# Second attention of a two-block transformer: wider score products, one compressed product, values' products of a query tile in one run

## The chip, the cores and the metric

The kernel runs on one core of a Trainium2 chip. Its time is the device time of one execution in microseconds (us); the median of several executions is given. The core's engines run beside each other and meet at semaphores: TensorE (matrix products; PE in the profile, PEld its weight loads), VectorE (DVE), ScalarE (ACT), GpSimd (POOL) and SyncE (SP, which issues transfers).

## The reference, cut to what matters

Two transformer blocks on 512 tokens of width 1024, in float32. The first block (two attentions, a mixture of experts) is not touched. The second mixes a causal convolution with an attention of 16 heads in 4 groups of 4 heads; each group shares its keys and values, 64 wide. Each head has three branches, weighted by sigmoid gates: compressed keys (31 blocks), selected blocks and a window. With 512 tokens the selection and the window both come to plain causal attention over all earlier tokens, with keys and values of their own:

```python
g = jax.nn.sigmoid(gate_logits).reshape(B, S, 3, G, R, 1)
o = g[:, :, 0] * o_cmp + g[:, :, 1] * o_slc + g[:, :, 2] * o_win
```

where `o_slc` and `o_win` are, for each head, softmax(q k^T / 8 + bias of the distance, masked) v.

## The kernel before, in words

The function `mixer` holds the second block's mixing. It normalises the input (`two_norms`), projects it with weights that arrive by DMA and are split into a high and a low part (`load_w`, lines 94 to 100: one transfer, one ACT and one DVE instruction), and multiplies with three products per 128 features (`mm3`, lines 84 to 86; in the trace `pz<-hh,whi`, `pz<-hl,whi`, `pz<-hh,wlo`, 512 columns each). These projections give queries, keys, values, gates and the inputs of the convolution. The convolution is done on DVE as 31 taps for each of 8 channel tiles (`taps`, lines 1490 and 1492), a few at a time between other work.

The attention loop (lines 1685 to 1707) goes over 8 units u: group g = u // 2 and pair pr = u % 2 of its heads. `k_stacks` writes the keys of two groups as stacked high and low parts, `KS[b][g][x]`, each 128 x 512, for branch b (0 selected, 1 window); it runs before unit 0 and again before unit 4, into the same memory. `cmp_branch` makes the compressed branch's probabilities `cpT` for a group. `attend` (line 1631) then works through four query tiles t of 128 tokens, with n = 128 (t + 1) visible keys, and yields after each one, so that taps, a gate of the convolution, a gate of the attention or the next group's queries are put in between in the program. In one tile:

- Scores: for each branch b and head i two products (lines 1643 and 1644) of n columns into a PSUM tile `sc` (two such tiles); DVE adds the bias and takes the minimum (line 1646) into `probs[b]`; ACT takes the exponential and its sum (line 1648). `probs` has one tile for each branch with two buffers each.
- In a block of raised priority, DVE turns sums and gates into factors (lines 1651 to 1654). Two products a tile (line 1658) put the compressed values into the output `po`, one for each head, in plain fp32 and of 128 columns.
- Then for each branch: for each head ACT scales the probabilities (line 1664), TensorE transposes their t + 1 blocks into a PSUM tile `tr` (line 1667; two such tiles), ACT copies them out to `aT` (line 1669; four buffers); then the branch's 2 (t + 1) products of values (line 1673), plain fp32, add to `po`. Head 0 writes rows 0 to 63 of `po`, head 1 rows 64 to 127.

After tile 3 DVE copies `po` out (line 1677); there is one `po`.

Nobody writes the order of an engine's instructions by hand. It is fixed when the kernel is built: of the instructions whose inputs are ready by its estimates, an engine takes the one that comes first in the program, and `high_priority(30)` moves a block's instructions ahead by 30 places. Each engine then runs its list in that order and waits where a semaphore is not yet there. `issue_after(x)` adds to that the rule that the block's instructions on the engine of x come behind x.

Of the kernel before, what the change touches and what calls it, by code (L numbers as in the profile page):

```python
# [1433 lines left out]
def mixer(K, X, vecd, gain, mem, pre, mem_done, wp):  # L1434
# [5 lines left out]
    with ExitStack() as st:  # L1440
# [56 lines left out]
        with ExitStack() as sk:  # L1497
# [5 lines left out]
            KS = [[None] * 4 for b in range(2)]  # L1503
# [6 lines left out]
            def k_stacks(j):  # L1510
                for b, c0 in ((0, 3584), (1, 4096)):
                    pz = proj(c0 + P * j)
                    for i in range(2):
                        KS[b][2 * j + i] = [kv.tile([P, S], F32R, tag=f"K{b}{i}{x}", bufs=1, name=K.uid("K")) for x in range(2)]
                        stack_k(K, pz, i, *KS[b][2 * j + i])
                    early()
# [114 lines left out]
            def attend(g, pr, qs, bt, cpT):  # L1631
                po = pso.tile([P, S], F32, tag="po", name=K.uid("po"))
                for t in range(NT):
# [3 lines left out]
                    probs = [wk.tile([P, 2, S], F32, tag=f"p{i}", name=K.uid("p")) for i in range(2)]  # L1637
                    m = wk.tile([P, 2, 2, 2], F32, tag="am", name=K.uid("am"))
                    for b in range(2):
                        for i in range(2):  # L1640
                            r = 2 * pr + i
                            sc = psc.tile([P, S], F32, tag="sc", name=K.uid("sc"))
                            nc.tensor.matmul(sc[:, :n], qs[r][:, ts_], KS[b][g][0][:, :n], start=True, stop=False)  # L1643
                            nc.tensor.matmul(sc[:, :n], qs[r][:, ts_], KS[b][g][1][:, :n], start=False, stop=True)  # L1644
                            p = probs[b][:, i, :n]
                            v.tensor_tensor_reduce(p, sc[:, :n], bt[r][:, b0:b0 + n], scale=1.0, scalar=3e38,  # L1646
                                                   op0=OP.add, op1=OP.min, accum_out=m[:, 0, b, i:i + 1])
                            nc.scalar.activation(p, p, AF.Exp, scale=-1.0, bias=m[:, 0, b, i:i + 1],  # L1648
                                                 accum_out=m[:, 1, b, i:i + 1])
                    with K.tc.high_priority(30):  # L1650
# [5 lines left out]
                        for i in range(2):  # L1656
                            r = 2 * pr + i
                            nc.tensor.matmul(po[64 * i:64 * i + 64, ts_], vcz[:, g, r, :], cpT[:, ts_], start=(t == 0),  # L1658
                                             stop=False, skip_group_check=True)
                        for b in range(2):  # L1660
                            pts = []
                            for i in range(2):
                                p = probs[b][:, i, :n]
                                nc.scalar.activation(p, p, AF.Copy, scale=m[:, 1, b, i:i + 1])  # L1664
                                pt = pst.tile([P, NT, P], F32, tag="tr", name=K.uid("tr"))
                                for k in range(t + 1):
                                    nc.tensor.transpose(pt[:, k, :], p[:, k * P:(k + 1) * P], K.ident)  # L1667
                                x = wk.tile([P, NT, P], F32, tag="aT", bufs=4, name=K.uid("aT"))
                                nc.scalar.activation(x[:, :t + 1], pt[:, :t + 1], AF.Copy)
                                pts.append(x)  # L1670
                            for k in range(t + 1):
                                for i in range(2):
                                    nc.tensor.matmul(po[64 * i:64 * i + 64, ts_], V[b][:, k, 64 * g:64 * g + 64],  # L1673
                                                     pts[i][:, k, :], start=False, stop=(b == 1 and k == t and t == NT - 1),
                                                     skip_group_check=True)
# [299 lines left out]
```

## Time and profile before

| what | value |
|---|---|
| median of 3 runs | 1972.51 us |
| lowest and highest | 1968.85 and 1977.4 us |
| the profiled execution's own time | 1969.21 us |
| its span, first to last instruction | 1967.4 us |
| mean granted TensorE clock | 0.989 of full speed |
| busy: TensorE products, DVE, ACT, POOL | 1907.5, 1093.7, 770.4, 156.3 us |

The profile comes from one execution. Busy time of TensorE counts every product from its start to a modelled end, and those overlap, so it says when TensorE had something in flight and not how full it was. What a product takes of TensorE's time is read from the distance between starts in the timeline.

### The profile page before, as it was taken

Reading aid. Unit: us, or ns where it says so; the run is one execution under the profiler, and the core shown is the slowest. Engines: PE = TensorE matmul, PEld = TensorE weight load, DVE = VectorE, ACT = ScalarE, POOL = GpSimd, SP = SyncE. Lnnn points to the kernel's source line nnn. Section 1 sums busy time; section 2 is a strip of 40 time slices with the busy share of each in tenths; the row PEclk is TensorE's granted clock in tenths of the full one; section 3 lists DMA queues with packets and bytes.
Section 4 is the critical chain, followed back from the end, with each engine's and each line's share of the span. In section 5 each row is a group of like instructions: output and inputs, shape, how many; then the busy total and the mean of one; then the engine's idle time right before and its main releaser. Section 6 shows DMA issues by size and latency. Waiting matters only on the chain.

```text
span 1967.4 us, 26583 instructions
## 1 busy us (share of the span) xinstructions
PE 1907.5 (97%) x10370; PEld 1395.2 (71%) x10370; DVE 1093.7 (56%) x1965; ACT 770.4 (39%) x1602; POOL 156.3 (8%) x226
## 2 busy tenths in 40 slices
PE   7999998899999999989999999999999999999998
PEld 5786678545455554548777777777898898888886
DVE  6876753722332223246998989747555544444423
ACT  5435653221112211124236776786344443332321
POOL 0111000000000000000011101101100001111000
PEclk8999999999999999999999999999999999999999
DMA  9854054699999999953332122202342133333322
GB/s 308 305 181 146 1 200 177 237 412 405 419 402 422 413 404 408 426 177 87 97 108 54 54 55 65 55 22 75 97 130 85 47 93 97 97 97 96 126 78 86
DMA packets 210327, 356.38 MB, mean 181 GB/s; under 512 B 18742, under 2 KB 160434, under 8 KB 185624
## 3 DMA queue, kind: packets, MB, share of 16 engines
q1 hardware_dynamic: 207168, 346.81, 48.7%
q0 software_dynamic: 2768, 7.75, 1.3%
q8 instruction: 83, 1.36, 0.3%
q14 instruction: 44, 0.36, 0.1%
q10 hardware_dynamic: 264, 0.10, 0.0%
HBM read 350.37 MB, written 9.49 MB: 183 GB/s over the span
## 4 chain that ended last, share of the span: by engine, by line
PE 47%; DVE 6%; issue 1%; ACT 1%; DMA 0%; POOL 0%; DVEq 0%; POOLq 0%; SPq 0%; ACTq 0%
PE pz L86 12%; PE pz L85 12%; PE pz L84 12%; PE po L1673 3%; PE tr L1667 2%; DVE cva L1492 2%; DVE wlo L100 1%; PE sc L1643 1%; PE sc L1644 1%; PE po L1658 0%; DMA xkr<-xkd 0%; PE tr L1328 0%; PE tr L1277 0%; DVE q L241 0%; DVE K L251 0%
## 5 line engine op out<-in xcount | busy, mean ns | idle before, releaser
L84 PE MATMUL pz<-hh,whi 128*128 128x512 f32 x912 | 362.8, 398 | 1.9 <-DVE cblk L1397 0.8
L86 PE MATMUL pz<-hh,wlo 128*128 128x512 f32 x912 | 360.4, 396 | 0.7 <-DVE wlo L100 0.7
L85 PE MATMUL pz<-hl,whi 128*128 128x512 f32 x912 | 359.7, 395 | 0.0
L99 ACT ACTIVATE whi<-raw 128x1024 fp32r<-128x1024 f32 (+2 forms) x166 | 181.2, 1096 | 346.1 <-PE pz L85 254.1
L100 DVE TENSOR_TENSOR wlo<-raw,whi 128x1024 fp32r<-128x1024 f32 (+2 forms) x166 | 219.5, 1326 | 77.9 <-ACT whi L99 77.6
L1094 PE MATMUL eg<-ew,xg 128*64 128x512 f32 x1024 | 224.3, 593 | 0.0
L84 PEld LDWEIGHTS pz<-hh,whi 128*128 128x128 f32 x912 | 171.4, 188 | 38.4 <-issue 2.1
L86 PEld LDWEIGHTS pz<-hh,wlo 128*128 128x128 f32 x912 | 171.6, 188 | 37.2 <-issue 2.1
L85 PEld LDWEIGHTS pz<-hl,whi 128*128 128x128 f32 x912 | 171.6, 188 | 35.3 <-issue 2.5
L1492 DVE SCALAR_TENSOR_TENSOR cva<-cv,cvp,cva 128x512 f32<-128x512 f32 x240 | 179.1, 758 | 4.2
L1094 PEld LDWEIGHTS eg<-ew,xg 128*64 128x64 f32 x1024 | 72.8, 137 | 142.3 <-issue 136.9
L1126 PE MATMUL ey<-ew,hT 128*64 128x512 f32 x512 | 115.1, 603 | 0.7 <-ACT hT L1115 0.7
L1131 DVE TENSOR_TENSOR yg<-ey,gate 128x512 f32<-128x512 f32 x32 | 22.1, 691 | 136.2 <-PE ey L1126 134.6
L1126 PEld LDWEIGHTS ey<-ew,hT 128*64 128x64 f32 x512 | 35.7, 138 | 70.2 <-issue 67.3
L1015 ACT ACTIVATE xg<-px,norm2s 128x128 f32<-128x128 f32 x128 | 48.2, 457 | 89.5 <-PE px L1010 89.5
L1132 ACT ACTIVATE yh<-yg 128x512 fp32r<-128x512 f32 x32 | 20.2, 630 | 149.9 <-DVE yg L1131 149.9
L1648 ACT ACTIVATE p<-p,am 128x128 f32<-128x128 f32 (+3 forms) x128 | 71.0, 559 | 20.0 <-DVE am L1646 17.0
L1646 DVE CUSTOM_DVE_ANT_0 p<-sc,bias 128x128 f32<-128x128 f32 (+3 forms) x128 | 60.0, 487 | 31.0 <-PE sc L1644 20.1
L1664 ACT ACTIVATE p<-p,am 128x128 f32<-128x128 f32 (+3 forms) x128 | 64.1, 554 | 13.3 <-DVE am L1654 13.1
L84 PE MATMUL pz<-whi,gh 128*128 128x512 f32 x176 | 68.5, 389 | 0.0
L85 PE MATMUL pz<-wlo,gh 128*128 128x512 f32 x176 | 68.5, 389 | 0.0
L86 PE MATMUL pz<-whi,gl 128*128 128x512 f32 x176 | 68.5, 389 | 0.0
(491 smaller groups left out, 3580.6 us busy)
## 6 DMA issues: line engine op xcount, KB each, us to landing
ew<-in_w_expert_gate_dram SPq DMA_DIRECT2D x64, 1024.0 KB
ew<-in_w_expert_up_dram SPq DMA_DIRECT2D x64, 1024.0 KB
ew<-in_w_expert_down_dram SPq DMA_DIRECT2D x64, 1024.0 KB
raw<-in_w_in_dram SPq DMA_DIRECT2D x53, 512.0 KB
wada<-in_w_ada_dram SPq DMA_DIRECT2D x48, 512.0 KB
raw<-in_ffn_in_w_dram SPq DMA_DIRECT2D x44, 512.0 KB
raw<-in_ffn_out_w_dram SPq DMA_DIRECT2D x22, 512.0 KB
raw<-in_w_in_dram SPq DMA_DIRECT2D x8, 1024.0 KB
```

The source lines that it names most:

```text
L84: nc.tensor.matmul(out, wh, hh, start=first, stop=False, **kw)
L85: nc.tensor.matmul(out, wh, hl, start=False, stop=False, **kw)
L86: nc.tensor.matmul(out, wl, hh, start=False, stop=last, **kw)
L99: nc.scalar.activation(hi[:, r], raw[:, r], AF.Copy)
L100: nc.vector.tensor_tensor(lo[:, r], raw[:, r], hi[:, r].bitcast(F32), op=OP.subtract)
L1094: nc.tensor.matmul(self.pz[64 * i:64 * i + 64], self.xg[:, k, 64 * i:64 * i + 64], next(self.rows_[i]), start=(k == 0), stop=(k == ND - 1))
L1126: nc.tensor.matmul(pys[c][64 * i:64 * i + 64], self.hT[:, k, 64 * i:64 * i + 64], wr[i][:, 512 * c:512 * c + 512], start=(k == 0), stop=(k ...
L1492: v.scalar_tensor_tensor(acc, cv[:, j:j + S], cvp[:, c, j:j + 1], acc, op0=OP.mult, op1=OP.add)
L1646: v.tensor_tensor_reduce(p, sc[:, :n], bt[r][:, b0:b0 + n], scale=1.0, scalar=3e38, op0=OP.add, op1=OP.min, accum_out=m[:, 0, b, i:i + 1])
L1648: nc.scalar.activation(p, p, AF.Exp, scale=-1.0, bias=m[:, 0, b, i:i + 1], accum_out=m[:, 1, b, i:i + 1])
L1664: nc.scalar.activation(p, p, AF.Copy, scale=m[:, 1, b, i:i + 1])
L1673: nc.tensor.matmul(po[64 * i:64 * i + 64, ts_], V[b][:, k, 64 * g:64 * g + 64], pts[i][:, k, :], start=False, stop=(b == 1 and k == t and ...
```

## The change

The keys' stacks get the two branches side by side: `KS[g][x]` is 128 x 2 x 512. For query tiles 0 and 1 one pair of products makes a head's scores against both branches (2n columns, 256 and 512) into one `sc` tile; DVE and ACT still work on each branch by itself, now head by head. Tiles 2 and 3 keep a pair for each branch and head. The buffers of `probs` are three under one tag instead of two for each branch, those of `aT` six instead of four. The compressed values are added for all 512 columns at tile 0, one product for each head. The transposes of several heads share a `tr` tile and one copy: four heads at tile 0, two at tile 1, one at tiles 2 and 3. The products of values of both branches come after all four heads' transposes, and `issue_after` keeps them behind the last transpose.

```diff
--- before.py
+++ after.py
@@ -1500,7 +1500,7 @@
             kcl = kv.tile([P, 4, P], F32R, name="kcl")
             vcz = kv.tile([P, 4, 4, 64], F32, name="vcz")
             gates = kv.tile([P, NT, 48], F32, name="gates")
-            KS = [[None] * 4 for b in range(2)]
+            KS = [None] * 4
             V = [kv.tile([P, NT, 256], F32, name=f"V{b}") for b in range(2)]
             gp.memset(kch.bitcast(F32), 0.0)
             gp.memset(kcl.bitcast(F32), 0.0)
@@ -1508,11 +1508,12 @@
             wq = sk.enter_context(tc.tile_pool(name="m_q", bufs=2, reuse_waits="tile"))
 
             def k_stacks(j):
+                for i in range(2):
+                    KS[2 * j + i] = [kv.tile([P, 2, S], F32R, tag=f"K{i}{x}", bufs=1, name=K.uid("K")) for x in range(2)]
                 for b, c0 in ((0, 3584), (1, 4096)):
                     pz = proj(c0 + P * j)
                     for i in range(2):
-                        KS[b][2 * j + i] = [kv.tile([P, S], F32R, tag=f"K{b}{i}{x}", bufs=1, name=K.uid("K")) for x in range(2)]
-                        stack_k(K, pz, i, *KS[b][2 * j + i])
+                        stack_k(K, pz, i, *(k[:, b] for k in KS[2 * j + i]))
                     early()
 
             def q_stacks(g):
@@ -1634,45 +1635,52 @@
                     ts_ = slice(t * P, (t + 1) * P)
                     n = P * (t + 1)
                     b0 = 384 - P * t
-                    probs = [wk.tile([P, 2, S], F32, tag=f"p{i}", name=K.uid("p")) for i in range(2)]
+                    probs = [wk.tile([P, 2, S], F32, tag="p", bufs=3, name=K.uid("p")) for i in range(2)]
                     m = wk.tile([P, 2, 2, 2], F32, tag="am", name=K.uid("am"))
-                    for b in range(2):
+                    together = 2 if t < 2 else 1
+                    for b in range(0, 2, together):
                         for i in range(2):
                             r = 2 * pr + i
                             sc = psc.tile([P, S], F32, tag="sc", name=K.uid("sc"))
-                            nc.tensor.matmul(sc[:, :n], qs[r][:, ts_], KS[b][g][0][:, :n], start=True, stop=False)
-                            nc.tensor.matmul(sc[:, :n], qs[r][:, ts_], KS[b][g][1][:, :n], start=False, stop=True)
-                            p = probs[b][:, i, :n]
-                            v.tensor_tensor_reduce(p, sc[:, :n], bt[r][:, b0:b0 + n], scale=1.0, scalar=3e38,
-                                                   op0=OP.add, op1=OP.min, accum_out=m[:, 0, b, i:i + 1])
-                            nc.scalar.activation(p, p, AF.Exp, scale=-1.0, bias=m[:, 0, b, i:i + 1],
-                                                 accum_out=m[:, 1, b, i:i + 1])
+                            for x in range(2):
+                                nc.tensor.matmul(sc[:, :together * n], qs[r][:, ts_], KS[g][x][:, b:b + together, :n],
+                                                 start=(x == 0), stop=(x == 1))
+                            for j in range(together):
+                                p = probs[b + j][:, i, :n]
+                                v.tensor_tensor_reduce(p, sc[:, j * n:j * n + n], bt[r][:, b0:b0 + n], scale=1.0,
+                                                       scalar=3e38, op0=OP.add, op1=OP.min,
+                                                       accum_out=m[:, 0, b + j, i:i + 1])
+                                nc.scalar.activation(p, p, AF.Exp, scale=-1.0, bias=m[:, 0, b + j, i:i + 1],
+                                                     accum_out=m[:, 1, b + j, i:i + 1])
                     with K.tc.high_priority(30):
                         v.tensor_scalar(m[:, 1], m[:, 1], 1e-30, None, op0=OP.max)
                         v.reciprocal(m[:, 1], m[:, 1])
                         h0 = 4 * g + 2 * pr
                         v.tensor_tensor(m[:, 1], m[:, 1],
                                         gates[:, t, 16:48].rearrange("p (b h) -> p b h", h=16)[:, :, h0:h0 + 2], op=OP.mult)
-                        for i in range(2):
-                            r = 2 * pr + i
-                            nc.tensor.matmul(po[64 * i:64 * i + 64, ts_], vcz[:, g, r, :], cpT[:, ts_], start=(t == 0),
-                                             stop=False, skip_group_check=True)
-                        for b in range(2):
-                            pts = []
+                        if t == 0:
                             for i in range(2):
+                                nc.tensor.matmul(po[64 * i:64 * i + 64], vcz[:, g, 2 * pr + i, :], cpT, start=True,
+                                                 stop=False, skip_group_check=True)
+                        heads, turned = [(b, i) for b in range(2) for i in range(2)], {}
+                        together = (4, 2, 1, 1)[t]
+                        for h in range(0, 4, together):
+                            pt = pst.tile([P, NT, P], F32, tag="tr", name=K.uid("tr"))
+                            x = wk.tile([P, NT, P], F32, tag="aT", bufs=6, name=K.uid("aT"))
+                            for j, (b, i) in enumerate(heads[h:h + together]):
                                 p = probs[b][:, i, :n]
                                 nc.scalar.activation(p, p, AF.Copy, scale=m[:, 1, b, i:i + 1])
-                                pt = pst.tile([P, NT, P], F32, tag="tr", name=K.uid("tr"))
                                 for k in range(t + 1):
-                                    nc.tensor.transpose(pt[:, k, :], p[:, k * P:(k + 1) * P], K.ident)
-                                x = wk.tile([P, NT, P], F32, tag="aT", bufs=4, name=K.uid("aT"))
-                                nc.scalar.activation(x[:, :t + 1], pt[:, :t + 1], AF.Copy)
-                                pts.append(x)
-                            for k in range(t + 1):
-                                for i in range(2):
-                                    nc.tensor.matmul(po[64 * i:64 * i + 64, ts_], V[b][:, k, 64 * g:64 * g + 64],
-                                                     pts[i][:, k, :], start=False, stop=(b == 1 and k == t and t == NT - 1),
-                                                     skip_group_check=True)
+                                    last = nc.tensor.transpose(pt[:, j * (t + 1) + k, :], p[:, k * P:(k + 1) * P], K.ident)
+                                turned[b, i] = x[:, j * (t + 1):(j + 1) * (t + 1)]
+                            nc.scalar.activation(x[:, :together * (t + 1)], pt[:, :together * (t + 1)], AF.Copy)
+                        with tc.issue_after(last.ins):
+                            for b in range(2):
+                                for k in range(t + 1):
+                                    for i in range(2):
+                                        nc.tensor.matmul(po[64 * i:64 * i + 64, ts_], V[b][:, k, 64 * g:64 * g + 64],
+                                                         turned[b, i][:, k], start=False,
+                                                         stop=(b == 1 and k == t and t == NT - 1), skip_group_check=True)
                     if t == NT - 1:
                         v.tensor_copy(nsa[:, 2 * g + pr, :], po)
                     yield
```

## Rows read from the trace of the kernel before

**Rows 1.** The page, its first lines: span, then busy us, share and instructions.
```profile
span 1967.4 us, 26583 instructions
...
PE 1907.5 (97%) x10370; PEld 1395.2 (71%) x10370; DVE 1093.7 (56%) x1965; ACT 770.4 (39%) x1602; POOL 156.3 (8%) x226
```

**Rows 2.** Stretches: length; busy us (count) PE, PEld, DVE, ACT, POOL; clock, DMA, GB/s.
```profile
1032.10:1248.00 215.90, 212.49 (x1326) 159.35 (x1325) 192.90 (x435) 150.27 (x372) 24.38 (x51) 0.99 0.22 59
1248.00:1341.30 93.30, 92.90 (x643) 68.07 (x642) 52.46 (x171) 78.77 (x210) 3.62 (x10) 1.00 0.11 30
1341.30:1967.40 626.10, 615.92 (x3173) 523.58 (x3171) 302.04 (x415) 216.58 (x349) 56.35 (x48) 1.00 0.31 94
```

**Rows 3.** Instructions by line, 1032 to 1341 us: count, busy us, mean ns, idle before.
```profile
L1673 PE MATMUL po<-aT,V 128*64 128x128 f32 x640 | 63.7, 285 | 0.8 <-ACT aT L1669 0.7
```

**Rows 4.** TensorE's timeline, a run of sixteen and one of four: start us, us.
```profile
1181.19 0.40 PE L86 MATMUL pz<-hh,wlo 128*128 128x512 f32 x1
1181.52 0.88 PE L1673 MATMUL po<-aT,V 128*64 128x128 f32 x12
1182.22 0.39 PE L1658 MATMUL po<-cpT,vcz 128*64 128x128 f32 x4
1182.54 0.51 PE L1643 MATMUL sc<-K,q 128*128 128x512 f32 x1
...
1312.74 0.44 PE L1673 MATMUL po<-aT,V 128*64 128x128 f32 x4
1313.11 0.33 PE L1667 MATMUL tr<-ident,p 128*128 128x128 f32 x1
```

**Rows 5.** The same timeline, a run that is broken after two records.
```profile
1338.12 0.40 PE L84 MATMUL pz<-hh,whi 128*128 128x512 f32 x1
1338.36 0.40 PE L85 MATMUL pz<-hl,whi 128*128 128x512 f32 x1
1338.68 0.43 PE L1673 MATMUL po<-aT,V 128*64 128x128 f32 x2
1339.05 0.50 PE L86 MATMUL pz<-hh,wlo 128*128 128x512 f32 x1
1339.48 1.09 PE L1673 MATMUL po<-aT,V 128*64 128x128 f32 x14
1340.49 0.50 PE L84 MATMUL pz<-hh,whi 128*128 128x512 f32 x1
```

**Rows 6.** The same timeline, the first of 39 lone products.
```profile
1049.54 0.43 PE L1673 MATMUL po<-aT,V 128*64 128x128 f32 x2
```

**Rows 7.** ACT's copies of transposed blocks by shape, 1032 to 1341 us.
```profile
L1669 ACT ACTIVATE aT<-tr 128x512 f32<-128x512 f32 x32 | 17.4, 593 | 5.3 <-PE tr L1667 5.2
...
L1669 ACT ACTIVATE aT<-tr 128x256 f32<-128x256 f32 x32 | 10.6, 381 | 2.1 <-PE tr L1667 1.5
...
L1669 ACT ACTIVATE aT<-tr 128x128 f32<-128x128 f32 x32 | 8.2, 275 | 5.0 <-PE tr L1667 4.7
```

**Rows 8.** Waits, 1032 to 1341 us: total us, times, longest us.
```profile
PEld po L1673 <- ACT aT L1669: 19.3, 55, 1.0
```

**Rows 9.** TensorE's timeline, scores of 128 columns (tile 0) and of 256 (tile 1).
```profile
1251.74 0.33 PE L1643 MATMUL sc<-K,q 128*128 128x128 f32 x1
...
1252.24 0.44 PE L84 MATMUL pz<-hh,whi 128*128 128x512 f32 x1
...
1254.06 0.29 PE L1644 MATMUL sc<-K,q 128*128 128x256 f32 x1
1254.19 0.28 PE L1643 MATMUL sc<-K,q 128*128 128x256 f32 x1
```

**Rows 10.** The page, costliest groups: the experts' fp32 products of 512 columns.
```profile
L1094 PE MATMUL eg<-ew,xg 128*64 128x512 f32 x1024 | 224.3, 593 | 0.0
```

**Rows 11.** Timeline in unit 6: DVE's second reduction of tile 1, TensorE's transposes of tile 0.
```profile
1285.55 0.39 DVE L1646 CUSTOM_DVE_ANT_0 p<-sc,bias 128x256 f32<-128x256 f32 x1
...
1290.85 0.27 PE L1667 MATMUL tr<-ident,p 128*128 128x128 f32 x1
```

## The prediction

> **What bounds the kernel now.** I read the page first: one core, a span of 1967.4 us, with a matrix product in flight in 1907.5 us of it [rows 1]. Then the busy time by stretch, with the attention loop as stretches of its own: its eight units (a unit is one pair of heads over four query tiles) run from 1032.1 to 1341.3 us. The reader should compare the engines row by row. TensorE is busy in 212.49 of the 215.90 us of units 0 to 4 and in 92.90 of the 93.30 us of units 5 to 7. DVE has 192.90 us of work in the first stretch (89%) and 52.46 in the second (56%); ACT has 70% and 84% [rows 2]. After the loop TensorE stays busy in 615.92 of 626.10 us with DVE under half, so what the loop saves should reach the end unshortened. TensorE bounds the loop, with DVE close behind in its first two thirds and ACT close behind in its last third.
>
> A full row says nothing about how much of TensorE's time is needed, because other projections fill every wait. So I read its timeline by start times. Each plain fp32 product stands in the trace as two records: 8 units of 40 products of values make 320, and the group has 640 records [rows 3]. Four records (one product for each of two heads, which write different halves of the output's rows) take 0.37 us from the first start to the next instruction (1312.74 to 1313.11) [rows 4]; sixteen take 1.02 us (1181.52 to 1182.54) [rows 4]. So four more cost (1.02 - 0.37) / 3 = 0.22 us, and leaving such a run costs 0.37 - 0.22 = 0.15 us. Entering costs too: the run starts 0.33 us after a projection (1181.19 to 1181.52) [rows 4], where the next projection would start 0.24 us after (1338.12 to 1338.36) [rows 5]. Call it 0.1. A run costs 0.25 us beside its content.
>
> Worse is a run that begins with one lone product, because the other head's probabilities are not yet copied. In rows 5 the same sixteen records stand as two, a projection, and fourteen: 2.13 us from 1338.36 to 1340.49, of which two projections are 0.24 each. The products took 1.65 us where the whole run takes 1.02 + 0.1 = 1.12: a lone product costs 0.53 us. Counting the timeline between the first and last of them, I find 103 runs of values' and compressed products in the loop, and 39 of them are a lone product; the first is at 1049.54 and the last at 1338.68 [rows 5, 6].
>
> **The change part by part.**
>
> **Values in one run.** All products of a query tile now queue behind its last transpose. Ideally 4 runs a unit plus one for the compressed values remain: 40 instead of 103, none with a lone start. The lone starts are worth 39 x 0.5 = 19.5 us and the other 24 runs 24 x 0.25 = 6 us. I do not take all of it: the last head's copy still ends after the last transpose, and a run can break there. I take 30 lone starts (15 us) and 16 runs (4 us); the ends are 0 and 25.5. The new wait: the run now stands behind the tile's last copy, of 0.28 to 0.59 us [rows 7], with only the first branch's products (0.22 us for each key block) ahead of it; behind it on TensorE queue the next tile's scores and the projections, and for the unit's last run DVE waits to take the output. At 0.59 us for 32 tiles that is at most 19 us, which is what TensorE already waits for those copies, 19.3 us [rows 8]; the difference counts as nothing.
>
> **Scores.** At tile 0 four products of 128 columns take 0.50 us (1251.74 to 1252.24) [rows 9], eight 1.0; after the change four of 256 columns do it, at 0.13 us each (1254.06 to 1254.19) [rows 9], 0.52. That is about 0.45 us a unit, 3.6 us in all. At tile 1 eight of 256 become four of 512, at 0.24 us as in a projection: 1.0 against 0.96, nothing. Here one row argues against a page. The trace shows 128 columns costing as much as 256. The Trainium skill, TensorE: Matmul & The Clock Gate, section Back-to-back issue gap, lists 134 cycles for 128 columns and 262 for 256, by which tile 0 would gain 8 x 134 - 4 x 262 = 24 cycles, 0.01 us a unit, and the TensorE sum below would be 19.0 instead of 22.6; no row here shows that pace at 128 columns.
>
> **Compressed values.** Per unit sixteen records of 128 columns (4 x 0.22 = 0.88 us) become four of 512. The nearest row, the expert products of the same 64-column shape, has 224.3 / 1024 = 0.22 us a record [rows 10], which gives 0.88 again: I take nothing. If the two heads' halves overlap as the narrow ones do, it is 0.44 a unit, 3.5 us; a wide one that overlapped nothing and was paced worse than that row is excluded by that row.
>
> **Transposes and copies.** The transposes stay 320. ACT's copies at tile 0 go from 4 x 0.275 to one of 0.593, at tile 1 from 4 x 0.381 to 2 x 0.593 [rows 7]: 0.85 us a unit, 6.8 in all. ACT has idle time, so this counts as nothing; in units 5 to 7, with ACT at 84%, it is 2.6 us of room. A tile of the keys' stacks now covers both branches; its second filling is written long after the scores that read the first, behind whole projections, so nothing.
>
> **The sum on TensorE**: 15 + 4 + 3.6 = 22.6 us; ends 3.6 and 19.5 + 6 + 3.6 + 3.5 = 32.6.
>
> **What of it arrives.** In units 0 to 4 DVE has 215.90 - 192.90 = 23.0 us idle, and none of its work goes. Five eighths of the sum, 14.1 us, would push DVE to 96%, in a stretch where each reduction still waits for a score. I take half, 7.0. In units 5 to 7 the share is 8.5 us and ACT and DVE have room (14.5 and 40.8 us); I take 7.0. Together 14.0 us. The profiled execution took 1969.21 us (span 1967.4 and 1.8 around it): 1955.2. The median of the runs shown is 3.3 us above that execution, so on the median's scale the forecast is 1958.5 us.
>
> **The rivals.** **DVE takes it all** where it is nearly full: only units 5 to 7 gain, 7 us, 1965.5. For it: 89% busy, an average over waits it cannot use. Against: the optional convolution taps can fill gaps or move into units 5 to 7.
>
> **The change does not do what it says**: the order on each engine is fixed when the kernel is built, by priorities, so a late copy may still let a projection or a transpose break into the run. Then mostly the scores' 3.6 us remain, 4 us: 1968.5.
>
> **Slower, by probability buffers.** Each branch had two; now the branches share three. At tiles 0 and 1 a head's two branches are reduced one after the other, so the second reduction of a tile needs the buffer that the first branch of the tile before still holds until its transposes. In unit 6 tile 1's second reduction starts at 1285.55, while tile 0's second transpose (first branch) starts at 1290.85 and takes 0.27 us [rows 11]: it would move by 5.6 us, with the tile's exponentials on ACT and what DVE has queued behind it. There are two such places a unit, 16 in all. DVE's and ACT's other work covers some; TensorE's gain of 14 us is gone when each costs 0.9 us net. At 2 us net (a third of 5.6) it is 32 - 14 = 18 us longer: 1990.5. Against: the first reduction needs no wait, and in units 0 to 4 taps stand ready. The Trainium skill, Perfetto Trace Analysis, section Optimization Strategy, says that the same gap repeating can mean too few buffers for the next tile; the rows show no such gap yet, as there are four.
>
> **Everything arrives**: DVE follows, runs are whole and the wide products overlap: 25 us or more, 1947 and below.
>
> **How the numbers follow.** About 0.5% (9.9 us) is what a measurement can tell from no change. Forecast 0.50 (its own range 1950 to 1965), DVE 0.17, not done 0.15, buffers 0.13, everything 0.05. Over 0.5% faster: 0.43 of the forecast, 0.04 of the DVE case and the last case, 0.52. Slower: 0.13, nearly all buffers. The rest, 0.35, within. The range 1947 to 1978 leaves out about 0.04 below and 0.11 above.
>
> **What would show it.** The loop should last about 295 us instead of 309.2, with transposes and products of values unchanged in number (320 and 640 records), scores 192 records instead of 256 and compressed products 32 instead of 128. Runs of values' products should be near 50, with few lone starts. DVE should stand at 92% or more in units 0 to 4. Wrong would be: as many runs as before; DVE's reductions waiting for transposes at tiles 0 and 1 in every unit; a loop of the same length with longer waits of ACT; or the loop shorter and what follows it longer.

## The result, and the profile after

The changed kernel takes 1953.06 us (median of 4 runs, 1951.51 to 1953.56) beside 1972.36 us (4 runs) of the kernel before: a ratio of 0.99, with a 95% interval of 0.9878 to 0.9921. That is 19.3 us, or 1.0%, less; the forecast was 14 us less, and the time lies inside the range given. The profiled execution took 1953.35 us.

The page of the changed kernel, its first lines (as in [rows 1]):

```profile
span 1951.6 us, 26213 instructions
...
PE 1886.8 (97%) x10210; PEld 1383.2 (71%) x10210; DVE 1090.7 (56%) x1965; ACT 765.2 (39%) x1562; POOL 153.5 (8%) x226
```

The stretches that answer to [rows 2], with the same columns; the loop now runs from 1034.4 to 1327.7 us (before: 1032.1 to 1341.3), and unit 4 ends at 1235.3:

```profile
1034.40:1235.30 200.90, 196.98 (x1232) 151.26 (x1230) 191.05 (x434) 146.77 (x347) 21.54 (x51) 1.00 0.24 64
1235.30:1327.70 92.40, 90.59 (x613) 68.03 (x612) 54.65 (x174) 76.18 (x193) 3.56 (x9) 1.00 0.15 41
1327.70:1951.60 623.90, 611.79 (x3138) 519.35 (x3136) 298.80 (x413) 217.42 (x351) 56.60 (x48) 0.99 0.30 92
```

Units 0 to 4 fell from 215.9 to 200.9 us with DVE's work nearly unchanged (192.90 to 191.05), so DVE went from 89% to 95%. The last stretch is shorter only by 2.2 us. Units 5 to 7 seem to have gained little (93.3 to 92.4), but something else happened there: the whole loop now holds 600 projection products where it held 564. Thirty-six of them, at 0.23 us each some 8.3 us, came in from behind the loop: 7 into units 0 to 4 and 29 into units 5 to 7. With them counted, TensorE saved some 24 us in the loop, not 15.9.

TensorE's lines in the loop, by shape (count, busy us, mean ns, idle before), beside [rows 3]:

```profile
L1674 PE MATMUL tr<-ident,p 128*128 128x128 f32 x320 | 53.0, 276 | 1.3 <-ACT p L1672 1.3
L1681 PE MATMUL po<-aT,V 128*64 128x128 f32 x640 | 45.5, 279 | 0.0
L1646 PE MATMUL sc<-K,q 128*128 128x512 f32 x96 | 32.4, 422 | 1.8 <-DVE am L1650 1.8
L1646 PE MATMUL sc<-K,q 128*128 128x384 f32 x64 | 17.2, 363 | 0.2 <-DVE am L1650 0.2
L1663 PE MATMUL po<-cpT,vcz 128*64 128x512 f32 x32 | 9.7, 617 | 0.0
L1646 PE MATMUL sc<-K,q 128*128 128x256 f32 x32 | 6.8, 305 | 0.0
```

The counts are the forecast ones: 320 and 640 as before, 96 + 64 + 32 = 192 records of scores, 32 of compressed values. The 640 records of values are in flight for 45.5 us instead of 63.7 [rows 3].

TensorE's timeline at the last tile of unit 7 (start us, us), and at a compressed product:

```profile
1324.43 0.60 PE L1674 MATMUL tr<-ident,p 128*128 128x128 f32 x4
1324.96 1.97 PE L1681 MATMUL po<-aT,V 128*64 128x128 f32 x32
1326.86 0.50 PE L86 MATMUL pz<-hh,wlo 128*128 128x512 f32 x1
```

```profile
1074.70 1.08 PE L1663 MATMUL po<-cpT,vcz 128*64 128x512 f32 x4
1075.71 0.50 PE L85 MATMUL pz<-hl,whi 128*128 128x512 f32 x1
```

All 32 records of this tile stand in one run, 1.90 us from its start to the next instruction: 8 x 0.22 + 0.15, the prices of [rows 4]. The four wide compressed records take 1.01 us; without the 0.15 of leaving that is 0.86, about what four narrow groups of four take. Counted as in [rows 5], the loop now has 46 runs, 2 of them with a lone start, where it had 103 and 39. The two are wide compressed products of one head each; the first is followed by a projection at 1236.56:

```profile
1235.56 1.07 PE L1663 MATMUL po<-cpT,vcz 128*64 128x512 f32 x2
1236.56 0.51 PE L85 MATMUL pz<-hl,whi 128*128 128x512 f32 x1
```

One head alone takes 1.00 us and both heads together 1.01, so the two heads' products, which write different halves of the output's rows, run at the same time. The narrow ones do the same: a lone product takes 0.36 us (the one of [rows 6], up to the transpose behind it), and [rows 4] has 0.37 for both heads:

```profile
1049.90 0.33 PE L1667 MATMUL tr<-ident,p 128*128 128x128 f32 x1
```

That is why a lone start is dear: it takes as long as the pair, and at the end of its run a product of the other head is left alone in the same way (the fourteen records behind the broken start of [rows 5] end with two that start 0.11 us apart, where the records of a pair start 0.01 us apart).

Waits of the loop (total us, times, longest us); the second line answers to [rows 8]:

```profile
DVE p L1650 <- PE tr L1674: 8.0, 8, 2.2
...
PEld po L1681 <- ACT aT L1676: 2.5, 9, 0.4
```

TensorE's waits for the copies fell from 19.3 to 2.5 us. A wait that was not there before is DVE's for the transposes, which free a probability buffer: 8.0 us in 8 places.

At the loop's start the change removes a stall. In the kernel before, tile 0 of unit 0 needs four score tiles, one after the other, and there are two; TensorE waits 1.44 us for a reduction on DVE, and then its granted clock falls to 0.50 (the level of 1.2 GHz), with projections 0.43 us apart. First TensorE's timeline before, then 5 us of the kernel before and the same 5 us of the changed one, from 4 us behind the loop's start on (columns as in [rows 2]):

```profile
1034.42 0.39 PE L84 MATMUL pz<-hh,whi 128*128 128x512 f32 x1
1036.24 0.33 PE L1643 MATMUL sc<-K,q 128*128 128x128 f32 x1 [1.44 <-DVE am L1646]
...
1038.07 0.63 PE L84 MATMUL pz<-hh,whi 128*128 128x512 f32 x1
1038.49 0.63 PE L85 MATMUL pz<-hl,whi 128*128 128x512 f32 x1
```

```profile
1036.00:1041.00 5.00, 4.76 (x17) 3.84 (x18) 4.73 (x21) 3.41 (x13) 0.53 (x1) 0.66 0.00 0
1038.40:1043.40 5.00, 4.54 (x20) 3.44 (x19) 5.00 (x19) 4.03 (x14) 0.46 (x1) 1.00 0.00 0
```

By the usual distances between starts the wait costs 1.6 us there and the clock 1.7 (an estimate). The changed kernel waits 0.30 and 0.46 us in this place, and its clock stays at 1.00. It is the joint scores that make the difference: the five kernels of this text whose scores stand apart at tile 0 (before, 1, 5, 8, 10) have 0.66 in these 5 us, and the nine others 1.00.

Right behind the loop there is a new stall, of the same kind. The timeline of TensorE, ACT and DVE (start us, us, then in brackets the idle time before and what ended it):

```profile
1333.11 0.39 PE L86 MATMUL pz<-hh,wlo 128*128 128x512 f32 x1
1334.10 0.63 ACT L1730 ACTIVATE sq<-cva 128x512 f32<-128x512 f32 x1 [0.72 <-POOL csum L1732]
1335.44 0.63 ACT L1730 ACTIVATE sq<-cva 128x512 f32<-128x512 f32 x1 [0.71 <-POOL csum L1732]
1335.44 2.28 DVE L1732 TENSOR_TENSOR csum<-csum,sq 128x512 f32<-128x512 f32 x3 [5.26 <-POOL csum L1732]
1335.98 1.06 ACT L1244 ACTIVATE eg<-pz 128x512 f32<-128x512 f32 x2
...
1336.61 0.79 PE L84 MATMUL pz<-hh,whi 128*128 128x512 f32 x1 [3.11 <-ACT eg L1244]
...
1340.08 0.63 PE L84 MATMUL pz<-hh,whi 128*128 128x512 f32 x1
...
1340.51 0.63 PE L85 MATMUL pz<-hl,whi 128*128 128x512 f32 x1
```

And the stretches around it, columns as in [rows 2]:

```profile
1332.00:1337.00 5.00, 1.89 (x8) 1.31 (x7) 1.38 (x2) 2.83 (x7) 3.25 (x3) 0.86 0.28 83
1337.00:1341.00 4.00, 4.00 (x8) 2.01 (x8) 2.92 (x9) 1.47 (x3) 0.00 (x0) 0.50 0.15 22
1341.00:1342.40 1.40, 1.40 (x5) 1.11 (x4) 0.19 (x2) 0.00 (x0) 0.96 (x2) 0.50 1.04 310
1342.40:1345.00 2.60, 2.60 (x15) 2.17 (x14) 0.05 (x1) 0.60 (x1) 0.27 (x1) 1.00 0.04 11
```

The normalisation of the convolution's output sums eight squares (line 1732, the first four sums on POOL, the last three on DVE). POOL takes 1.3 us for a sum where DVE takes 0.8 (2.28 / 3), ACT's squares wait for them one by one, ACT's copy `eg` stands behind the squares in ACT's list, and only that copy frees the PSUM tile for TensorE's next projection. TensorE is idle for 3.1 us, and then its granted clock stands at 0.50 until about 1342.4, some 6 us of work: projections follow each other at 0.43 us instead of 0.23. In the kernel before, TensorE waits for nothing right behind the loop: from 1340.84 to 1343.39 its projections start every 0.23 us.

One more thing is needed to compare single executions. What lies ahead of the attention moves from run to run by several us, whatever the kernel. The first copy of the second block's values, in the kernel before and in the changed one:

```profile
932.88 0.60 ACT L1531 ACTIVATE vT<-pz 128x512 f32<-128x512 f32 x1
```

```profile
935.17 0.60 ACT L1532 ACTIVATE vT<-pz 128x512 f32<-128x512 f32 x1
```

From the end of that copy to the end of the span it is 1967.4 - 933.5 = 1033.9 us before and 1951.6 - 935.8 = 1015.8 after: 18.1 us less. Two executions of the old attention, whose programs differ only in the engine of four sums behind the loop, gave 1033.9 and 1033.8 (experiment 8), so this distance, called D below, is used beside the medians. It is read from one execution of each kernel. Measured from the changed kernel, D and the medians below agree within 2 us, except for no_order (4.2 by D, 7.6 by the medians). D splits at the end of DVE's last copy of `po`: 407.8 + 626.1 before, 391.9 + 623.9 after. A part of that split is always which projections stand in the loop, so their number is given too, at 0.23 us each.

### The profile page after: what moved, and what is told of

Its sections match the earlier page's. It is cut to its first block, busy times and chain, and to the rows that moved or that the text cites. A ratio compares the mean times of both kernels' runs of the same rounds, so it can differ in the third digit from the quotient of the medians.

```text
span 1951.6 us, 26213 instructions
## 1 busy us (share of the span) xinstructions
PE 1886.8 (97%) x10210; PEld 1383.2 (71%) x10210; DVE 1090.7 (56%) x1965; ACT 765.2 (39%) x1562; POOL 153.5 (8%) x226
```

## The experiments

The theory to be tested: the gain is the whole runs, it arrives because TensorE and not DVE bounds the loop, and some of it is given back in the stall. Rivals: the other parts carry it; DVE kept half of it; the three probability buffers cost what the prediction feared. All results together (us; runs, lone starts and projections counted in the loop):

| kernel | median, ratio and interval | D: to loop's end + rest | runs, lone | projections |
|---|---|---|---|---|
| before | 1972.36 | 407.8 + 626.1 = 1033.9 | 103, 39 | 564 |
| changed | 1953.06, 0.99 (0.9878-0.9921) | 391.9 + 623.9 = 1015.8 | 46, 2 | 600 |
| 1 run_only | 1956.49, 0.9921 (0.9908-0.9933) | 391.3 + 627.3 = 1018.6 | 58, 6 | 556 |
| 2 scores_only | 1968.32, 0.9984 (0.9974-0.9994) | 407.8 + 622.1 = 1029.9 | 105, 43 | 583 |
| 3 no_order | 1960.66, 0.9941 (0.9928-0.9954) | 401.3 + 618.7 = 1020.0 | 71, 4 | 608 |
| 4 tail_dve | 1948.86, 0.9875 (0.9861-0.9889) | 391.7 + 619.0 = 1010.7 | 46, 2 | 600 |
| 5 scores_apart | 1951.13, 0.9904 (0.9886-0.9923) | 394.0 + 618.5 = 1012.5 | 47, 4 | 594 |
| 6 cmp_per_tile | 1947.8, 0.9878 (0.986-0.9896) | 391.4 + 617.8 = 1009.2 | 46, 4 | 605 |
| 7 copy_per_head | 1958.78, 0.9933 (0.9919-0.9946) | 401.3 + 618.5 = 1019.8 | 61, 5 | 613 |
| 8 before_tail | 1970.87, 0.9993 (0.9981-1.0005) | 407.8 + 626.0 = 1033.8 | 103, 39 | 564 |
| 9 probs_four | 1946.63, 0.9873 (0.9858-0.9888) | 386.3 + 622.7 = 1009.0 | 49, 8 | 582 |
| 10 light_before_tail | 1973.35, 1.0007 (0.9994-1.0021) | 409.0 + 626.1 = 1035.1 | 103, 38 | 562 |
| 11 light_after_tail | 1946.14, 0.987 (0.9848-0.9893) | 384.2 + 623.9 = 1008.1 | 48, 6 | 564 |
| 12 four_tile_tail | 1947.34, 0.9878 (0.986-0.9895) | 385.6 + 622.8 = 1008.4 | 54, 9 | 580 |

### 1 and 2. The run alone, the scores alone

Run_only keeps of the change only the order of the values' products; scores_only is the tile of the kernel before with joint scores. Both have four probability buffers, two for each branch.

```diff
 run_only, against the changed kernel
-                    probs = [wk.tile([P, 2, S], F32, tag="p", bufs=3, name=K.uid("p")) for i in range(2)]
+                    probs = [wk.tile([P, 2, S], F32, tag=f"p{i}", name=K.uid("p")) for i in range(2)]
-                    together = 2 if t < 2 else 1
+                    together = 1
...
-                        if t == 0:
-                            for i in range(2):
-                                nc.tensor.matmul(po[64 * i:64 * i + 64], vcz[:, g, 2 * pr + i, :], cpT, start=True,
...
+                        for i in range(2):
+                            nc.tensor.matmul(po[64 * i:64 * i + 64, ts_], vcz[:, g, 2 * pr + i, :], cpT[:, ts_],
...
-                        together = (4, 2, 1, 1)[t]
+                        together = 1
...
-                            x = wk.tile([P, NT, P], F32, tag="aT", bufs=6, name=K.uid("aT"))
+                            x = wk.tile([P, NT, P], F32, tag="aT", bufs=4, name=K.uid("aT"))
```

```diff
 scores_only, against the kernel before
...
-                    for b in range(2):
+                    together = 2 if t < 2 else 1
+                    for b in range(0, 2, together):
...
-                            nc.tensor.matmul(sc[:, :n], qs[r][:, ts_], KS[b][g][0][:, :n], start=True, stop=False)
-                            nc.tensor.matmul(sc[:, :n], qs[r][:, ts_], KS[b][g][1][:, :n], start=False, stop=True)
+                            for x in range(2):
+                                nc.tensor.matmul(sc[:, :together * n], qs[r][:, ts_], KS[g][x][:, b:b + together, :n],
+                                                 start=(x == 0), stop=(x == 1))
```

> The changed kernel with only the run of values' products kept (all four heads' transposes first, then the products behind the last of them); scores for each branch, compressed values for each tile, a copy for each head and the buffers as before. My theory, that runs without lone starts are most of the gain: 45 to 60 runs in the loop, at most 6 lone starts, and 1956 to 1962 us. Rival, that shared copies on ACT or the joint scores bring the gain: 1967 to 1973 us although the runs are as few.

> The kernel before with only the joint scores of tiles 0 and 1. My theory, 3.6 us less of TensorE's time, half of which arrives: 1968 to 1971 us, with about 100 runs and 35 to 45 lone starts. Rival, that joint scores free the score tiles and so remove TensorE's waits: 1958 to 1965 us.

Both came out as the theory had it, run_only with 58 runs and 6 lone starts. D fell by 15.3 us with the run alone and by 4.0 with the scores alone. Neither kernel has the stall behind the loop (from 1327.8 to 1341 us TensorE is busy throughout in run_only, at a granted clock of 1.00), so they are to be measured against the 23.2 us that the change brings without it (experiment 4). The run is the change's core, with two thirds of that. Together with the scores it is 19.3 us, and the 3.9 left are about what the shared copies are worth (experiment 7). The rival of scores_only is right in one place: at the loop's start the joint scores do remove a wait and a fall of the clock. The 4.0 us are therefore not the products' content alone, and that they lie so near the 3.6 forecast is in part luck.

### 3. Without the rule of order

```diff
-                        with tc.issue_after(last.ins):
+                        if True:
```

> The changed kernel without the rule that values' products come behind the last transpose; the program still lists them after the transposes. If the rule makes the runs: 70 to 100 runs and 1960 to 1967 us. If the place in the program is enough: 46 to 55 runs and 1952 to 1955 us.

The rule makes the runs: 71 of them and 1960.66 us are both inside the first range, if at its lower end. D is 1020.0, which is 9.3 us more than tail_dve, the kernel with the rule and, like this one, without a fall of the clock behind the loop. Even without the rule most lone starts are gone (4 left), presumably because the values' products of both branches stand behind all transposes in the program; the rule joins the rest.

### 4 and 8. The sums of squares on DVE, in both kernels

```diff
-                    (v if c > 4 else gp).tensor_tensor(csum, csum, sq, op=OP.add)
+                    v.tensor_tensor(csum, csum, sq, op=OP.add)
```

> The changed kernel with all seven sums of squares after the loop on DVE (before: four on POOL, three on DVE). Theory, that some of the gain is given back there, where TensorE stands 3.1 us behind ACT and its clock then falls to 0.5 for about 4 us: neither stands in the trace any more and the time is 1947 to 1950 us. Rival, that the stretch hides behind other work: 1952 to 1954 us.

> The kernel before with all seven sums of squares after the loop on DVE. Theory, that the wait behind ACT there came only with the change, which pulls more projections into the loop: 1970 to 1974 us, and within 1 us of the 1033.9 us of the kernel before from the first copied values to the end. Rival, that the sums on POOL cost both kernels the same: 1966 to 1969 us.

The same edit takes 5.1 us off the changed kernel (D 1015.8 to 1010.7) and nothing off the kernel before (1033.9 to 1033.8; the ratio's interval contains 1). So the stall came with the change, and it cost 5.1 us; without it the change brings 1033.9 - 1010.7 = 23.2 us. In tail_dve seven sums run on DVE in one piece, and TensorE's clock stays at 1.00 in the stretches behind the loop, which ends there at 1334.9:

```profile
1337.32 5.47 DVE L1732 TENSOR_TENSOR csum<-csum,sq 128x512 f32<-128x512 f32 x7
```

```profile
1334.90:1339.00 4.10, 4.10 (x20) 3.39 (x19) 3.31 (x5) 3.92 (x7) 0.00 (x0) 1.00 0.09 10
1339.00:1344.00 5.00, 4.47 (x18) 3.10 (x17) 4.51 (x6) 3.33 (x6) 0.00 (x0) 1.00 0.33 98
```

### 5 and 6. The changed kernel with one part undone: scores, compressed values

```diff
 scores_apart
-                    together = 2 if t < 2 else 1
+                    together = 1
 cmp_per_tile
-                        if t == 0:
-                            for i in range(2):
-                                nc.tensor.matmul(po[64 * i:64 * i + 64], vcz[:, g, 2 * pr + i, :], cpT, start=True,
-                                                 stop=False, skip_group_check=True)
+                        for i in range(2):
+                            nc.tensor.matmul(po[64 * i:64 * i + 64, ts_], vcz[:, g, 2 * pr + i, :], cpT[:, ts_],
+                                             start=(t == 0), stop=False, skip_group_check=True)
```

> The changed kernel with the scores of tiles 0 and 1 in a product for each branch again. My theory, 3.6 us of TensorE's time and nearly all of it arriving: 1955.5 to 1958 us, and 3 to 5 us more from the first copied values to the end than the changed kernel's 1015.8. Rival, that the joint scores only gain where runs are broken: 1952 to 1954.5 us.

> The changed kernel with the compressed values added tile by tile again, 128 columns at a time. My theory, equal content (0.88 us a unit either way) and one more run in some tiles: 1953 to 1957 us, 50 to 70 runs. Rival, that the two heads' wide products overlap and save 3.5 us of content: 1957 to 1960 us.

Both expectations missed: each kernel came out faster than the changed one, by 3.3 and 6.6 us of D. The split shows why. The loop is not shorter in either by more than half a us (394.0 and 391.4 beside 391.9); the part behind it is, where TensorE's clock stays at 1.00 in both. Cmp_per_tile, the same place (compare 1.89 of 5.00 above):

```profile
1332.00:1337.00 5.00, 4.75 (x18) 3.23 (x18) 3.29 (x11) 1.91 (x3) 0.15 (x1) 1.00 0.03 4
```

So they have to be compared with tail_dve, which has no stall either: scores apart cost 1.8 us there, though the stall at the loop's start is back in this kernel, and the single compressed product saves nothing (cmp_per_tile is 1.5 us below). Differences of this size also contain which projections the order happened to pull into the loop, and are not told apart from that.

### 7. A copy for each head

```diff
-                        together = (4, 2, 1, 1)[t]
+                        together = 1
```

> The changed kernel with a transposed tile and a copy for each head in every query tile. My theory, 6.8 us more for ACT, which has idle time: 1952.5 to 1955 us. Rival, that ACT's copies set when runs start: 1957 to 1961 us.

The rival was right: D rose by 4.0 us, the runs from 46 to 61. By the distances between its starts, values' and compressed products take some 5 us more in the loop than in the changed kernel (63 beside 58). Behind the loop this kernel has a stall too (TensorE busy for 1.12 of 3 us), so it is compared with the changed kernel itself; its stall is shorter (2.6 us of idle time beside 3.1), but inside the loop it waits 2.4 us for a split weight where the changed kernel waits 1.5 us, so the 4.0 are good to one or two us. Its timeline shows where the last copy comes too late for the run in front of it:

```profile
1327.56 0.49 PE L1674 MATMUL tr<-ident,p 128*128 128x128 f32 x3
1327.99 1.09 PE L1681 MATMUL po<-aT,V 128*64 128x128 f32 x14
1329.00 0.50 PE L86 MATMUL pz<-hh,wlo 128*128 128x512 f32 x1
1329.44 0.87 PE L1681 MATMUL po<-aT,V 128*64 128x128 f32 x10
```

A tile of 24 records stands as 14 and 10 around one projection.

### 9. Four probability buffers

```diff
-                    probs = [wk.tile([P, 2, S], F32, tag="p", bufs=3, name=K.uid("p")) for i in range(2)]
+                    probs = [wk.tile([P, 2, S], F32, tag=f"p{i}", name=K.uid("p")) for i in range(2)]
-                            x = wk.tile([P, NT, P], F32, tag="aT", bufs=6, name=K.uid("aT"))
+                            x = wk.tile([P, NT, P], F32, tag="aT", bufs=4, name=K.uid("aT"))
```

> The changed kernel with two probability buffers for each branch again and four instead of six buffers for the copied blocks (the same memory). If the three shared buffers cost time (the slower rival at a low price): 1945 to 1950 us, and DVE's waits for transposes gone. If they are hidden: 1952 to 1955 us. If the two extra buffers for copied blocks carry a gain of their own: 1956 us or more.

D fell by 6.8 us, 5.6 of it in the loop. But 18 projections, 4.1 us of them, have moved out of the loop, so its own work is shorter only by some 1.5 us. DVE's wait for the transposes fell from 8.0 to 3.2 us, but another one, for ACT's scaling, grew to 10.6; the sum of DVE's waits does not show the price. Waits of the loop in this kernel:

```profile
DVE p L1650 <- ACT p L1672: 10.6, 4, 3.8
...
DVE p L1650 <- PE tr L1674: 3.2, 5, 1.2
```

Behind the loop this kernel waits 1.5 us, and the clock stays at 1.00, so it has to be compared with tail_dve too: the buffers' own price (three under one tag and six for the copies, against four and four) is not 6.8 us but 1.7 (1010.7 - 1009.0). The rest is the stall that is gone.

### 10 and 11. Less work for DVE

In both kernels, with the sums on DVE, every second tap of the convolution inside the loop is left out, so that DVE has less to do there.

```diff
-        waiting, convs = [], [0]
+        waiting, convs, light = [], [0], []
...
-                else:
+                elif not light or j % 2 == 0:
                     v.scalar_tensor_tensor(acc, cv[:, j:j + S], cvp[:, c, j:j + 1], acc, op0=OP.mult, op1=OP.add)
...
+            light.append(1)
             for u in range(ND):
```

> The kernel before with the sums on DVE, and with every second convolution tap left out inside the attention loop (those of odd number), which takes some 55 us from DVE there. If DVE bounds the loop of the kernel before: 1945 to 1960 us. If TensorE does: 1966 to 1973 us.

> The changed kernel with the sums on DVE and the same taps left out. The step of my prediction, that DVE keeps half of TensorE's saving in the first five units, makes the distance to the kernel before of the same kind grow from 23 us (with all taps) to 28 us or more. Rival, that DVE followed and nearly all arrived: the distance stays at 20 to 25 us.

Units 0 to 4, each kernel's own, in before_tail and then in light_before_tail, and in tail_dve and then in light_after_tail (columns as in [rows 2]):

```profile
1036.50:1252.40 215.90, 212.50 (x1325) 159.41 (x1324) 192.87 (x435) 150.18 (x372) 23.48 (x51) 0.99 0.22 59
```

```profile
1033.60:1250.20 216.60, 212.96 (x1329) 159.44 (x1328) 148.64 (x367) 150.32 (x372) 18.52 (x50) 0.99 0.22 59
```

```profile
1041.80:1242.60 200.80, 196.91 (x1232) 151.20 (x1230) 191.05 (x434) 146.75 (x347) 21.97 (x51) 1.00 0.24 64
```

```profile
1035.30:1232.70 197.40, 195.59 (x1226) 150.63 (x1225) 145.57 (x366) 146.17 (x347) 20.51 (x50) 1.00 0.23 63
```

DVE has over 40 us less to do in each. The kernel before does not gain (its median of 1973.35 us is just above the 1966 to 1973 expected if TensorE bounds it; D 1033.8 to 1035.1, and units 0 to 4 from 215.9 to 216.6): DVE did not bound it. The changed one gains 2.6 us (1010.7 to 1008.1): that is the most that DVE holds there at 95%. Where it holds them is not shown, since the loop is 7.5 us shorter but has 36 projections, 8.3 us, fewer. The distance between the two kernels is 23.1 us with all taps and 27.0 without (22.0 and 27.2 by the medians), between what the two expectations had put (20 to 25 and 28 or more): DVE keeps something, 2.6 us or by the distance 3.9, but not half.

### 12. The better variants together

Sums on DVE, four probability buffers, compressed values by tile: the edits of experiments 4, 6 and 9 in one.

> The changed kernel with three edits that were each faster alone: two probability buffers for each branch with four for copied blocks, compressed values tile by tile, and the sums on DVE. If their gains are of different places and add: 1937 to 1943 us. If they all only keep TensorE from running dry after the loop: 1945 to 1949 us.

They do not add up. D is 1008.4, as with four buffers alone (1009.0) or compressed values by tile alone (1009.2): each of the three had removed the stall. Beside tail_dve, two of the edits together bring 2.3 us. The four best medians of kernels that leave nothing out (1946.63, 1947.34, 1947.8, 1948.86) are below both kernels, 4 to 6 us below the changed one, and are not told apart.

## Why the prediction was right, and where it was off

**What bounds it** was right: TensorE bounds the loop (experiment 10 took 44 us from DVE in units 0 to 4, and nothing was gained).

**Values in one run** was right in mechanism and near in size. I took 30 lone starts and 16 runs, 19 us; 37 lone starts and 57 - 37 = 20 other runs went. Adding up the distances between starts over the loop, the fp32 products with their late entries cost about 79.2 us before and 58.0 after: 21.2 less, give or take 1 by what is called late. That the new wait behind the last copy costs nothing was right too: 2.5 us, where 19.3 stood.

**Scores**: 3.6 taken. By the same count scores cost 49.6 and then 44.2 us, 5.4 less; alone they brought 4.0 us of D. At tile 0 they went from 9.2 to 5.1 us, 4.1 less. At tile 1, where nothing was taken, they went from 9.8 to 8.2; 0.6 of that is the clock of 0.50 at the loop's start. The prediction had no term for that stall, 3.3 us with the projections in it. The rule of the Trainium skill that was weighed there (TensorE: Matmul & The Clock Gate, Back-to-back issue gap: 128 columns at about half the price of 256) would have left no gain from tile 0, and the 4.1 us speak against it for these products.

**Compressed values**: nothing taken, nothing found. The upper end was wrongly reasoned: the two heads' wide products do overlap (1.00 us for one head, 1.01 for both), and yet nothing is saved, because the 0.22 us a record that was taken from [rows 10] has the overlap of two products in it already. There too the records start in pairs, 0.01 us apart, with 0.42 us to the next pair.

**Copies on ACT** "counts as nothing": this step failed. As time of ACT they are worth nothing, but the shared copy comes early enough for the run to stay whole, and without it 15 runs more appear: about 4 us (experiment 7).

**The sum on TensorE**, 22.6 us, measured about 26.6 (21.2 + 5.4), within its ends of 3.6 and 32.6.

**What arrives** was mis-sized, and this is the step that made the forecast too small. I took half of 14.1 us in units 0 to 4 because DVE would reach 96%. DVE reached 95%, and that stretch still fell by 15.0 us, with 7 projections more in it: 16.6 us, five eighths of the 26.6. DVE held at most 2.6 to 3.9 us in all (experiment 11), not half of 14. Its 191 us of work fitted into the shorter stretch, because its waits could shrink as well (DVE's idle time there fell from 23.0 to 9.9 us).

**"What the loop saves should reach the end unshortened"** failed as well: 5.1 us were given back behind the loop (experiments 4 and 8). With the stall removed the change brings 23.2 us of D, of the 26.6 that TensorE's own products save. The two errors have opposite signs, 23.2 - 5.1 = 18.1 against the 14 forecast, so the total was closer than its parts; that much of the near hit is luck.

**The slower rival** exists, at a small price. The wait is of the kind that was named, DVE's reductions behind transposes, but in 8 places and not 16, only two of them at tiles 0 and 1, and at 1.0 us each and not 5.6. Four buffers bring 1.7 us beside tail_dve, so three cost far less than the change gains. The Trainium skill (Perfetto Trace Analysis, Optimization Strategy) says that the same gap repeating on the engine that should be saturated can mean too few buffers. No run here shows such a gap in every unit: the waits are DVE's, 8 of at most 2.2 us, and undoing the edit showed their price. **DVE takes it all** is refuted by experiment 11, and **the change does not do what it says** by the 46 runs.

**Open**: the order of an engine's list is fixed when the kernel is built, so each edit also moves projections in or out of the loop (556 to 613 of them), and can bring or remove a stall. The price of a single part below some 2 us is not known from these runs.

## What to carry to other kernels

Judge a full TensorE by the distances between starts and not by its busy time: broken runs of plain fp32 products cost some 21 us here, though TensorE stood idle for only 0.8 us before those products [rows 3]. Keeping a tile's products together behind its last transpose gave two thirds of the gain. A second engine at 95% need not hold the gain when its own idle time can shrink with the stretch. When two executions are compared stretch by stretch, start each stretch at the same instruction and count what has moved in or out. After shortening a stretch, look at what frees the PSUM tiles right behind it: work that used to be early enough may now stall TensorE.

## What was not expected of the hardware

Two plain fp32 products with 64 output rows each, which write different halves of the output's rows, run at the same time: both take 0.37 us together and one alone 0.36; at 512 columns it is 1.01 and 1.00. Inside a run the pair costs 0.22 us at 128 columns and about 0.86 at 512 (an estimate: 1.01 without the 0.15 of leaving), 4 times as much for 4 times the columns, so width brought nothing; what counts is that both heads' products stand next to each other.

A wait of 3.1 us of TensorE was followed by some 6 us at a granted clock of 0.50, with projections 0.43 us apart instead of 0.23, and the stall cost 5.1 us in all. At the loop's start of the kernel before, a wait of 1.44 us was followed by 3.6 us of that kind. The clock's part is in no row of waits.
